# Low halves of 56 weight tiles: an accumulating DMA onto ScalarE's negated high halves, in place of VectorE's subtraction

## The chip, the cores and the metric

The kernel runs on one core of a Trainium2 chip. Its engines have lists of their own and run side by side: TensorE (PE, with its weight load PEld), VectorE (DVE), ScalarE (ACT), GpSimd (POOL), SyncE (SP, which issues the loads). The metric is device time in microseconds. The profile is of one execution.

## The reference

One decoder block on 512 tokens of width 1024, float32. Three token mixers are fed by one projection, merged by sigmoid gates, projected, added; a gated MLP with a short causal convolution follows.

```python
h = rms_norm(x, ln1_g[l]);  z = h @ w_in[l]
z_a, z_b, z_c, z_g = jnp.split(z, split_at, axis=-1)
u, v = jnp.split(jax.nn.gelu(z_a), 2, axis=-1)
v = layer_norm(v, sg_ln_g[l], sg_ln_b[l])
y_a = (u * chunked_spatial_gating(v, sg_w[l], sg_b[l])) @ w_a_out[l]
p, g_lin = jnp.split(z_b, 2, axis=-1)
c = causal_depthwise_conv(p * jax.nn.sigmoid(g_lin), cv_w[l], cv_b[l])      # 31 taps
y_b = jax.nn.silu(layer_norm(c, cv_ln_g[l], cv_ln_b[l])) @ w_b_out[l]
q, k, vv = jnp.split(z_c, 3, axis=-1)                                       # q, k normalised per head
y_c = stick_breaking_attention(q, k, vv) @ w_c_out[l]                       # 8 heads of 64
gates = jax.nn.sigmoid(z_g.reshape(bsz, t, N_BRANCH, d) + b_gate[l])
merged = gates[:, :, 0] * y_a + gates[:, :, 1] * y_b + gates[:, :, 2] * y_c
x = x + merged @ w_out[l]
up = causal_depthwise_conv(rms_norm(x, ln2_g[l]) @ w_up[l], ffn_conv_w[l], ffn_conv_b[l])
gate, val = jnp.split(up, 2, axis=-1)
x = x + (jax.nn.silu(gate) * val) @ w_down[l]
```

## The kernel before

Each float32 matrix product is made of three products of shorter numbers. Every operand is split into a high half (`hi`, rounded to the type float32r) and a low half (`lo`, what the rounding left), and `mm3` issues high times high, high times low and low times high, all into one PSUM tile. A split (`split`) is a copy on ScalarE that rounds, and a subtraction on VectorE.

All weights lie in one array `wall` of 140 tiles of 128x1024, in the order of their use: 8 for the convolution branch's input (`NZB`), 20 for the token projections (`NTOK`: values and gates of the spatial gating, q, k, v), 24 for the gates (`NZG`) and 12 for the branch outputs (`NY`), these two mixed branch by branch, then 8, 44 and 24 for the output projection and the MLP. One weight tile feeds 24 matmuls. `wload` (line 156) fetches and splits a tile: SP loads it into one of two raw buffers (`wr`), ScalarE writes `wh`, VectorE `wl`, each into a buffer of a pool of six, so three weights are held at a time. The copy of weight i waits until PE is done with weight i - 3. `wnext` issues `wload` two weights ahead. Both instructions carry a high priority (`hot`) in the scheduler that puts the written program in its final order.

Work that is not a weight's product is written as generators in queues (`side`): the convolution's taps (`conv`, VectorE), the attention's scores, sigmoids and transposed operands (`soft`, ScalarE, VectorE and PE), its scans (`scan`, VectorE), the transposes and the product with v (`av`, PE, ScalarE and VectorE). A planner sets when they are written: `spend` adds the estimated cost of what was issued to a clock for each engine, and `fill`, called twice per weight, takes the next step of `soft` while the clocks of ScalarE and VectorE are behind PE's, and of `conv` while VectorE's is. A weight was charged `PEU`, `SPD` and `SPA` (PE, VectorE, ScalarE), in two halves. Every engine works off its list in order. POOL's list has the masks of the scores (the affine selects of line 650), which VectorE's line 690 waits for.

The weights 8 to 63 are used in `tok_group` (line 441) and `branch` (line 764). The functions that the change touches:

Of the kernel before, what the change touches and what calls it, by code (L numbers as in the profile page):

```python
# [11 lines left out]
AF = mybir.ActivationFunctionType  # L12
ALU = mybir.AluOpType
# [3 lines left out]
T = 512  # L17
# [21 lines left out]
NZB, NTOK, NZG, NY, NOUT, NUP, NDN = 8, 20, 24, 12, 8, 44, 24  # L39
# [6 lines left out]
def tile_block(ctx: ExitStack, tc: tile.TileContext, xT, x0g, wall, cst, lnv, sgw, outT):  # L46
    nc = tc.nc
    act, dve, pool, pe, sp = nc.scalar, nc.vector, nc.gpsimd, nc.tensor, nc.sync
# [37 lines left out]
    f = lambda ap: ap.bitcast(F32)  # L86
# [16 lines left out]
    def load(out, in_):  # L103
        i = sp.dma_start(out=out, in_=in_)
        after(i, dlast[0])
        dlast[0] = i.ins
# [8 lines left out]
    def split(hi, lo, src):  # L115
        act.copy(out=hi, in_=src)  # L116
        dve.tensor_tensor(out=lo, in0=src, in1=f(hi), op=ALU.subtract)  # L117
# [5 lines left out]
    def mm3(out, ah, al, bh, bl, start, stop, behind=None):  # L123
        i = pe.matmul(out=out, lhsT=ah, rhs=bh, start=start, stop=False)  # L124
        after(i, behind)
        mark[0] = i.ins
        pe.matmul(out=out, lhsT=ah, rhs=bl, start=False, stop=False)  # L127
        pe.matmul(out=out, lhsT=al, rhs=bh, start=False, stop=stop)  # L128
# [9 lines left out]
    def hot():  # L138

        return tc.high_priority(int(HOT * tc.cur_priority))  # L140
# [9 lines left out]
    state = {"next": 0}  # L150
# [2 lines left out]
    WARM = 6  # L153
    CONVF = 1.08

    def wload(i):
        n = 768 if i >= NW - NDN and (i - (NW - NDN)) % 3 == 2 else 1024
        raw = wr.tile([P, 1024], F32, tag="wr", name="wr")
        hi = ws.tile([P, 1024], F32R, tag="w", name="wh")
        lo = ws.tile([P, 1024], F32R, tag="w", name="wl")  # L160
        load(raw[:, :n], wall[i, :, :n])
        with hot():
            split(hi[:, :n], lo[:, :n], raw[:, :n])
        wq[i] = (hi, lo)

    def wnext(i):
        while state["next"] < min(NW, i + 1 + AHEAD):
            wload(state["next"])
            state["next"] += 1
        return wq.pop(i)  # L170
# [6 lines left out]
    def spend(pe=0.0, dve=0.0, act=0.0):  # L177
        clk["pe"] += pe
        clk["dve"] += dve
        clk["act"] += act  # L180
# [14 lines left out]
    def fill():  # L195
        for k in ("dve", "act"):
            clk[k] = max(clk[k], clk["pe"] - 10.0)
        live = {n: bool(side[n]) for n in side}
        while True:
            for n, need in (("hi", ()), ("av", ()), ("scan", ()), ("soft", ("act", "dve")), ("conv", ("dve",))):  # L200
                if live[n] and all(clk[k] < clk["pe"] for k in need):
                    live[n] = step(side[n])
                    break
            else:
                return
# [7 lines left out]
    def ca(n, s=0):  # L213
        return 0.09 + s * 0.09 + n * 0.000833

    def cd(n, s=0):
        return 0.07 + s * 0.06 + n * 0.001042
# [16 lines left out]
    for k in range(KD):  # L234
        i, j = k // 2, half[k % 2]
# [3 lines left out]
        raw, hi, lo = w4[i]  # L239
# [141 lines left out]
    def chan_unit(i, ps, xs):  # L381

        hi, lo = wnext(i)
        for k in range(KD):
            ks = slice(k * P, (k + 1) * P)
            mm3(ps, hi[:, ks], lo[:, ks], xs[k][0], xs[k][1], k == 0, k == KD - 1)
            if k == 3:
                spend(PEU / 2, SPD / 2, SPA / 2)
                fill()
        spend(PEU / 2, SPD / 2, SPA / 2)  # L390

    def group4():
        return [MM(), MM(), Z(), AV()]
# [1 line left out]
    PEU, SPD, SPA = 5.11, cd(1024), ca(1024)  # L395
# [4 lines left out]
    for kk in range(4):  # L400
        hi, lo = wnext(iw)
# [39 lines left out]
    def tok_group(evac, dve_c, act_c):  # L441
        nonlocal iw
        g = group4()
        for kk in range(4):
            hi, lo = wnext(iw)
            iw += 1

            order = [(c, j) for c in range(4) for j in range(2)] if kk == 3 else \
                [(c, j) for j in range(2) for c in range(4)]
            for n, (c, j) in enumerate(order):  # L450
                k = 2 * kk + j
                js = slice(j * 512, (j + 1) * 512)
                cs = slice(c * P, (c + 1) * P)
                xh, xl = xn[k][0][:, cs], xn[k][1][:, cs]
                pe.matmul(out=g[c], lhsT=xh, rhs=hi[:, js], start=k == 0, stop=False)  # L455
                pe.matmul(out=g[c], lhsT=xh, rhs=lo[:, js], start=False, stop=False)  # L456
                mark[0] = pe.matmul(out=g[c], lhsT=xl, rhs=hi[:, js], start=False, stop=k == KD - 1).ins  # L457
                if k == KD - 1:
                    with hot():
                        evac(c, g[c])  # L460
                if n == 3 or n == 7:
                    if n == 7 and kk == 3:
                        spend(0, dve_c, act_c)
                    spend(PEU / 2, SPD / 2, SPA / 2)
                    fill()


# [296 lines left out]
    def branch(b, src, need, first, last):  # L764
        nonlocal iw
        for half in range(2):
            gate = []
            for j in range(4):
                oc = half * 4 + j
                ps = MM()  # L770
                chan_unit(iw, ps, xn)
                iw += 1
                with hot():
                    gate.append(S())
                    table_act(out=gate[j], in_=ps, func=AF.Sigmoid, bias=c_("bg", b * 8 + oc))
                spend(0, 0, ca(T))
                fill()
            finish(*need)
            for i2 in range(2):
                hi, lo = wnext(iw)  # L780
                iw += 1
                for jj in range(2):
                    j = 2 * i2 + jj
                    oc = half * 4 + j
                    ps = MM()
                    for k in range(KW):
                        ks = slice((jj * KW + k) * P, (jj * KW + k + 1) * P)
                        mm3(ps, hi[:, ks], lo[:, ks], src[k][0], src[k][1], k == 0, k == KW - 1)
                    with hot():
                        dve.tensor_tensor(out=gate[j], in0=ps, in1=gate[j], op=ALU.mult)  # L790
                    if first:
                        m[oc] = gate[j]
                    else:
                        dve.tensor_tensor(out=m[oc], in0=m[oc], in1=gate[j], op=ALU.add)  # L794
                    if last:
                        mg[oc] = PR()
                        split(mg[oc][0], mg[oc][1], m[oc])
                    spend(PEU / 2, SPD / 2 + 2 * cd(T), SPA / 2)
                    fill()

    branch(0, uaT, ["hi"], True, False)
# [6 lines left out]
    for oc in range(KD):  # L808
        x1[oc] = S()
        sp.dma_start(out=x1[oc], in_=xT[oc])  # L810
        hi, lo = wnext(iw)
# [18 lines left out]
    for fch in range(KF):  # L830
        cv = []
        pss = []
        for gv in range(2):
            hi, lo = wnext(iw)
# [8 lines left out]
        for gv in range(2):  # L843
# [6 lines left out]
            for s in (1, 2):  # L850
                dve.scalar_tensor_tensor(out=a[:, :T - s], in0=t[:, s:T], scalar=c_("fw", ch * 3 + s),  # L851
                                         in1=a[:, :T - s], op0=ALU.mult, op1=ALU.add)
# [12 lines left out]
    for oc in range(KD):  # L865

        w = {}
        for n in ((slice(0, T),) if oc < KD - 1 else (slice(0, T // 2), slice(T // 2, T))):
            ps = Z()
            for k in range(KF):  # L870
# [3 lines left out]
                hi, lo = w[k // 8]  # L874
# [99 lines left out]
```

## Time and profile before

| | us |
|---|---|
| median of 3 runs (811.57 to 812.11) | 811.88 |
| the profiled execution | 813.14 |
| its span | 810.6 |
| PE busy in the span | 801.5 |
| VectorE, ScalarE, POOL busy | 569.6, 365.6, 26.3 |

The span is the time from the first to the last instruction that the profile records; the rest of the execution lies around it. Busy shares are means over stages that differ: in the first 300 us VectorE is nearly full, later it is not. Matmuls overlap each other, so a row's duration of a matmul is longer than the distance from its start to that of the next.

### The profile page before, as it was taken

The page shows a single profiled execution, that of the slowest core. Times are in us where ns is not written, and L with a number is a line of the kernel's source. Part 1 is how long each engine was busy: PE and PEld are TensorE (multiplying, and loading weights), DVE is VectorE, ACT ScalarE, POOL GpSimd, SP SyncE. Part 2 cuts the span into 40 slices and gives each one's busy share as a digit, 9 for nine tenths or more (in the row PEclk, how much of TensorE's full clock was granted, in tenths as well). Part 3 has the DMA queues.
Part 4 walks back from the last instruction along what each step waited for, and adds up shares of the span by engine and source line. Part 5 has one row for each costly group of instructions (what it writes and reads, how often), then busy time and mean ns, then how long its engine had stood idle before and what let it go on. Part 6 is the DMA issues. An engine that isn't in the chain of part 4 may idle for free.

```text
span 810.6 us, 9429 instructions
## 1 busy us (share of the span) xinstructions
PE 801.5 (99%) x3672; PEld 665.0 (82%) x3672; DVE 569.6 (70%) x772; ACT 365.6 (45%) x526; POOL 26.3 (3%) x44
## 2 busy tenths in 40 slices
PE   9999999998999999999999999999999999999998
PEld 6888888877887888888888888888888888888888
DVE  7799988999899887955556777777777777322221
ACT  7354434687585533643434544444444444211110
POOL 0001000021121100000000000000000000000000
PEclk9999999999999999999999999999999999999999
DMA  7233332212212132232244233223223322333330
GB/s 268 79 128 133 103 102 66 94 55 76 77 54 78 53 105 82 100 104 82 101 168 135 87 104 103 82 102 104 97 85 105 104 84 92 111 104 130 104 105 27
DMA packets 24812, 80.49 MB, mean 99 GB/s; under 512 B 2752, under 2 KB 3392, under 8 KB 24768
## 3 DMA queue, kind: packets, MB, share of 16 engines
q1 hardware_dynamic: 24768, 79.89, 29.4%
q8 instruction: 29, 0.48, 0.3%
q14 instruction: 15, 0.12, 0.0%
HBM read 77.78 MB, written 2.10 MB: 99 GB/s over the span
## 4 chain that ended last, share of the span: by engine, by line
PE 89%; DVE 8%; ACT 2%; issue 1%; DVEq 0%
PE z L124 18%; PE z L127 18%; PE z L128 18%; PE mm L124 7%; PE mm L127 7%; PE mm L128 6%; PE mm L457 2%; PE mm L455 2%; PE mm L456 2%; DVE s L334 2%; DVE h L687 2%; DVE wl L117 2%; PE z L457 1%; PE z L455 1%; PE a L455 1%
## 5 line engine op out<-in xcount | busy, mean ns | idle before, releaser
L116 ACT CAST wh<-wr 128x1024 fp32r<-128x1024 f32 (+1 forms) x136 | 141.7, 1042 | 247.7 <-PE z L127 114.3
L124 PE MATMUL z<-s,wh 128*128 128x512 f32 (+1 forms) x617 | 236.2, 383 | 0.0
L128 PE MATMUL z<-s,wl 128*128 128x512 f32 (+1 forms) x617 | 236.2, 383 | 0.0
L127 PE MATMUL z<-s,wh 128*128 128x512 f32 (+1 forms) x617 | 236.2, 383 | 0.0
L117 DVE TENSOR_TENSOR wl<-wr,wh 128x1024 fp32r<-128x1024 f32 (+1 forms) x136 | 164.6, 1210 | 100.8 <-ACT wh L116 99.2
L128 PEld LDWEIGHTS z<-s,wl 128*128 128x128 f32 x617 | 116.0, 188 | 22.8
L124 PEld LDWEIGHTS z<-s,wh 128*128 128x128 f32 x617 | 116.0, 188 | 22.7
L127 PEld LDWEIGHTS z<-s,wh 128*128 128x128 f32 x617 | 116.0, 188 | 22.6
L124 PE MATMUL mm<-s,wh 128*128 128x512 f32 x302 | 120.5, 399 | 0.0
L127 PE MATMUL mm<-s,wh 128*128 128x512 f32 x302 | 118.2, 391 | 0.0
L128 PE MATMUL mm<-s,wl 128*128 128x512 f32 x302 | 117.7, 392 | 0.0
L334 DVE SCALAR_TENSOR_TENSOR s<-s,cst 128x511 f32<-128x511 f32 (+29 forms) x120 | 82.5, 732 | 1.5 <-ACT s L329 1.3
L128 PEld LDWEIGHTS mm<-s,wl 128*128 128x128 f32 x302 | 57.0, 189 | 12.3
L124 PEld LDWEIGHTS mm<-s,wh 128*128 128x128 f32 x302 | 57.2, 189 | 11.7 <-ACT s L113 0.5
L851 DVE SCALAR_TENSOR_TENSOR h<-h,cst 128x511 f32<-128x511 f32 x88 | 65.7, 747 | 1.5
L127 PEld LDWEIGHTS mm<-s,wh 128*128 128x128 f32 x302 | 57.2, 189 | 11.1 <-DVE s L117 0.2
L848 DVE TENSOR_TENSOR h<-z,rs 128x512 f32<-128x512 f32 x44 | 30.2, 687 | 39.9 <-PE z L128 39.8
L849 ACT ACTIVATE h<-h,cst 128x512 f32<-128x512 f32 x44 | 35.9, 816 | 3.2 <-DVE h L848 3.0
L116 ACT CAST s<-h 128x512 fp32r<-128x512 f32 x18 | 11.2, 620 | 49.1 <-DVE h L856 49.1
L113 ACT ACTIVATE h<-h 128x512 f32<-128x512 f32 x22 | 13.9, 632 | 42.1 <-DVE h L851 42.1
L116 ACT CAST s<-s 128x512 fp32r<-128x512 f32 x29 | 17.5, 620 | 31.9 <-DVE s L794 14.1
L455 PE MATMUL mm<-wh,s 128*128 128x512 f32 x80 | 31.3, 391 | 0.0
(187 smaller groups left out, 882.1 us busy)
## 6 DMA issues: line engine op xcount, KB each, us to landing
wr<-wall SPq DMA_DIRECT2D x128, 512.0 KB, 3.3
s<-xT SPq DMA_DIRECT2D x15, 256.0 KB, 4.1
wr<-wall SPq DMA_DIRECT2D x8, 384.0 KB, 3.0
outT<-s SPq DMA_DIRECT2D x7, 256.0 KB, 2.0
h<-wall SPq DMA_DIRECT2D x3, 512.0 KB, 7.0
s<-lnv SPq DMA_DIRECT2D x2, 256.0 KB, 3.6
s<-sgw SPq DMA_DIRECT2D x2, 256.0 KB, 3.6
x<-x0g SPq DMA_DIRECT2D x1, 260.0 KB, 2.7
```

Of the source, the lines that this page charges most:

```text
L116: act.copy(out=hi, in_=src)
L117: dve.tensor_tensor(out=lo, in0=src, in1=f(hi), op=ALU.subtract)
L124: i = pe.matmul(out=out, lhsT=ah, rhs=bh, start=start, stop=False)
L127: pe.matmul(out=out, lhsT=ah, rhs=bl, start=False, stop=False)
L128: pe.matmul(out=out, lhsT=al, rhs=bh, start=False, stop=stop)
L334: after(dve.scalar_tensor_tensor(out=acc[j][:, :T - s], in0=cc[j][:, s:], scalar=c_("cvw", j * TAPS + s), in1=acc[j][:, :T - s], op0=ALU.m ...
L455: pe.matmul(out=g[c], lhsT=xh, rhs=hi[:, js], start=k == 0, stop=False)
L456: pe.matmul(out=g[c], lhsT=xh, rhs=lo[:, js], start=False, stop=False)
L457: mark[0] = pe.matmul(out=g[c], lhsT=xl, rhs=hi[:, js], start=False, stop=k == KD - 1).ins
L848: dve.tensor_tensor(out=t[:, :T], in0=pss[gv], in1=rs2, op=ALU.mult)
L849: act.activation(out=a, in_=t[:, :T], func=AF.Identity, scale=c_("fw", ch * 3), bias=c_("fb", ch))
L851: dve.scalar_tensor_tensor(out=a[:, :T - s], in0=t[:, s:T], scalar=c_("fw", ch * 3 + s), in1=a[:, :T - s], op0=ALU.mult, op1=ALU.add)
```

## The change

For the 56 weights 8 to 63 the low half is made in another way. ScalarE writes the high half as before, then a second time with the factor -1 into the buffer of the low half. A DMA in POOL's queue reads the weight from HBM again and adds it to that buffer, so that it holds the weight less its high half. The other weights are split as before. The planner's charge for such a weight is 0 for VectorE and twice the old one for ScalarE.

```diff
+    def bydma(i):
+        return NZB <= i < NZB + NTOK + NZG + NY
+
+    def wspend():
+        if bydma(state["next"]):
+            spend(PEU / 2, 0, SPA)
+        else:
+            spend(PEU / 2, SPD / 2, SPA / 2)
...
         load(raw[:, :n], wall[i, :, :n])
         with hot():
-            split(hi[:, :n], lo[:, :n], raw[:, :n])
+            act.copy(out=hi[:, :n], in_=raw[:, :n])
+            if not bydma(i):
+                dve.tensor_tensor(out=lo[:, :n], in0=raw[:, :n], in1=f(hi[:, :n]), op=ALU.subtract)
+            else:
+                act.activation(out=lo[:, :n], in_=f(hi[:, :n]), func=AF.Copy, scale=-1.0)
+                pool.dma_start(out=lo[:, :n], in_=wall[i, :, :n], accum_op=ALU.add)
...
-                spend(PEU / 2, SPD / 2, SPA / 2)
+                wspend()
                 fill()
-        spend(PEU / 2, SPD / 2, SPA / 2)
+        wspend()
...
-                    spend(PEU / 2, SPD / 2 + 2 * cd(T), SPA / 2)
+                    wspend()
+                    spend(0, 2 * cd(T), 0)
                     fill()
```

The lists of the engines move with the planner. In the changed kernel the lines from `wload` on have higher numbers: the copy is L174, VectorE's subtraction L176, the negation L179, the DMA L180, and the lines behind them are 17 higher than before.

ScalarE's list before, in the middle of the attention's stage; `wh` is a weight's high half, `h` the scores' tiles, `s<-z` the split of transposed scores, `s<-mm` a gate's sigmoid:

```order
L116 CAST wh<-wr 128x1024
L116 CAST s<-z 128x128
L113 ACTIVATE s<-mm,cst 128x512
L113 ACTIVATE h<-z,qs 128x512 x2
L113 ACTIVATE h<-z,qs 128x384 x2
L113 ACTIVATE h<-z,qs 128x256 x2
L113 ACTIVATE h<-z,qs 128x128 x2
L116 CAST s<-z 128x512
L116 CAST s<-z 128x384
L116 CAST wh<-wr 128x1024
```

The same stage on ScalarE now; L179 writes the negated half, L371 squares for the convolution's layer norm:

```order
L174 CAST wh<-wr 128x1024
L116 CAST s<-z 128x128
L179 ACTIVATE wl<-wh 128x1024
L113 ACTIVATE s<-mm,cst 128x512
L116 CAST s<-z 128x512
L113 ACTIVATE h<-z,qs 128x512
L116 CAST s<-z 128x384
L113 ACTIVATE h<-z,qs 128x512
L113 ACTIVATE h<-z,qs 128x384 x2
L113 ACTIVATE h<-z,qs 128x256 x2
L113 ACTIVATE h<-z,qs 128x128 x2
L371 ACTIVATE s<-s 128x512 x2
```

The negation stands one to three instructions behind the copy, and the layer norm of the convolution, which stood behind the last head, is drawn into this stage.

POOL's list before, from the end of the start-up on:

```order
L273 MEMSET onesW 128x128
L491 AFFINE_SELECT s<-s 128x512 x2
L659 MEMSET s 128x512
L660 AFFINE_SELECT s<-s 128x128
L650 AFFINE_SELECT h<-h 128x128 x32
```

POOL's list now, from the end of the start-up to the masks of the fourth head (L667, before L650):

```order
L677 AFFINE_SELECT s<-s 128x128
L180 DMA wl<-wall 128x1024 x13
L667 AFFINE_SELECT h<-h 128x128
L180 DMA wl<-wall 128x1024
L667 AFFINE_SELECT h<-h 128x128 x3
L180 DMA wl<-wall 128x1024
L667 AFFINE_SELECT h<-h 128x128
L180 DMA wl<-wall 128x1024
L667 AFFINE_SELECT h<-h 128x128 x4
L180 DMA wl<-wall 128x1024
L667 AFFINE_SELECT h<-h 128x128 x3
```

The DMAs stand between the masks of each head; VectorE's list holds 56 subtractions less, and PE's holds the same matmuls, with the scores and transposes of the attention written earlier (the last head's transposes by about 17 us of PE's work).

## Rows read from the trace of the kernel before

**Rows 1.** The page's first lines: span; busy time and share of each engine.

```profile
span 810.6 us, 9429 instructions
PE 801.5 (99%) x3672; PEld 665.0 (82%) x3672; DVE 569.6 (70%) x772; ACT 365.6 (45%) x526; POOL 26.3 (3%) x44
```

**Rows 2.** Windows: length, busy (x) of PE, PEld, DVE, ACT, POOL, PEclk, DMA, GB/s.

```profile
30.00:150.00 120.00, 120.00 (x550) 100.08 (x549) 111.08 (x171) 56.33 (x82) 3.73 (x4) 1.00 0.30 101
...
180.00:210.00 30.00, 27.64 (x136) 22.75 (x134) 28.65 (x40) 22.80 (x46) 5.98 (x9) 0.94 0.22 71
...
480.00:600.00 120.00, 120.00 (x531) 99.36 (x530) 87.70 (x111) 54.17 (x67) 0.00 (x0) 1.00 0.29 97
153.85:279.39 125.54, 121.30 (x606) 100.60 (x605) 113.34 (x155) 87.19 (x164) 21.55 (x32) 0.99 0.21 68
154.00:248.00 94.00, 90.65 (x452) 74.86 (x451) 86.91 (x118) 70.49 (x131) 15.41 (x24) 0.98 0.20 66
```

**Rows 3.** Timeline of PE: start, duration, line, operation, tiles (x: instructions merged).

```profile
194.41 0.28 PE L713 MATMUL a<-s,b 128*128 128x256 f32 x1
194.53 0.28 PE L714 MATMUL a<-s,b 128*128 128x256 f32 x1
...
194.82 0.41 PE L700 MATMUL z<-ident,h 128*128 128x128 f32 x2
197.56 0.45 PE L700 MATMUL z<-ident,h 128*128 128x128 f32 x1 [2.33 <-DVE s L624]
...
241.31 0.93 PE L700 MATMUL z<-ident,h 128*128 128x128 f32 x7
241.99 0.47 PE L124 MATMUL mm<-s,wh 128*128 128x512 f32 x1
```

**Rows 4.** Chain of waits, 192 to 202: start, duration, engine, tile, line.

```profile
195.39 1.23 DVE wl L117
...
196.65 0.77 DVE s L624
...
198.00 0.43 PE mm L124
```

**Rows 5.** Groups by shape: count | busy us, mean ns | idle before, releasers.

```profile
L117 DVE TENSOR_TENSOR wl<-wr,wh 128x1024 fp32r<-128x1024 f32 x128 | 156.9, 1226 | 100.8 <-ACT wh L116 99.2
L116 ACT CAST wh<-wr 128x1024 fp32r<-128x1024 f32 x128 | 135.0, 1055 | 225.5 <-PE z L127 92.1 <-PE mm L127 44.1 <-issue 42.5
...
L113 ACT ACTIVATE h<-h 128x512 f32<-128x512 f32 x22 | 13.9, 632 | 42.1 <-DVE h L851 42.1
L116 ACT CAST s<-h 128x512 fp32r<-128x512 f32 x18 | 11.2, 620 | 49.1 <-DVE h L856 49.1
```

**Rows 6.** ScalarE's waits, 150 to 280: waiter, releaser: us in total, times, longest.

```profile
ACT s L116 <- DVE s L721: 5.7, 3, 2.8
...
ACT s L626 <- DVE s L624: 3.3, 3, 1.7
```

**Rows 7.** The page's DMA queue (share of 16 engines) and issues (us to landing).

```profile
q1 hardware_dynamic: 24768, 79.89, 29.4%
...
wr<-wall SPq DMA_DIRECT2D x128, 512.0 KB, 3.3
...
h<-wall SPq DMA_DIRECT2D x3, 512.0 KB, 7.0
```

**Rows 8.** Groups by shape, POOL.

```profile
L650 POOL TENSOR_SCALAR_AFFINE_SELECT h<-h 128x128 f32<-128x128 f32 x32 | 21.6, 682 | 173.9 <-ACT h L113 173.7
...
masks.py:199 POOL TENSOR_SCALAR_AFFINE_SELECT ident<-ident 128x128 f32<-128x128 f32 x1 | 0.3, 292 | 0.0
```

**Rows 9.** Timeline of ScalarE, casts of weights 28 and 29; in brackets the wait.

```profile
148.41 1.06 ACT L116 CAST wh<-wr 128x1024 fp32r<-128x1024 f32 x1 [1.81 <-PE a L456]
...
153.85 1.05 ACT L116 CAST wh<-wr 128x1024 fp32r<-128x1024 f32 x1 [4.00 <-PE a L456]
```

More of the change, by code (lines that the diff above doesn't have):

```diff
@@ L463, in tok_group @@
                         spend(0, dve_c, act_c)
-                    spend(PEU / 2, SPD / 2, SPA / 2)
+                    wspend()
                     fill()
@@ L797, in branch @@
                         split(mg[oc][0], mg[oc][1], m[oc])
-                    spend(PEU / 2, SPD / 2 + 2 * cd(T), SPA / 2)
+                    wspend()
+                    spend(0, 2 * cd(T), 0)
                     fill()
```

## The prediction, made before the changed kernel ran

> **What bounds the kernel now.** I read the page first. The profiled execution took 813.14 us with a span of 810.6, so 2.5 us lie around the span, and it stands 1.3 us above the median of 811.88. TensorE (PE) is busy for 801.5 of 810.6 us [rows 1]: no change on another engine can give back more than what PE loses somewhere. The table by stages says where that is [rows 2]. From 30 to 150 us, and from 480 to 600, PE is never idle; the later stretch has 531 matmuls in 120.00 us, a pace of 0.226 us for one of 512 columns. The loss lies between about 150 and 280, where the attention's scores, scans and transposes run beside the gates. From the cast of the 29th weight tile at 153.85 to that of the 45th at 279.39 are 125.54 us. In the order of before, PE's list between the matmuls that release these two casts holds 413 matmuls of 512 columns, 30 of 384, 30 of 256 and 124 of 128. The first cost 0.227; two of 256 start 0.12 apart, and seven transposes of 128 take from 241.31 to 241.99, 0.10 each, [rows 3]; I take 0.118 and 0.105, and 0.172 for 384 by interpolation. That is 115.5 us of work, so this stage loses 10.1 us. Of them 4.2 show as idle PE (121.30 busy), and some 1.8 as clock: the granted clock is 0.94 in 180 to 210 [rows 2]. The rest is matmuls that start late and overlap nothing.
>
> Why PE waits there is seen around 195: a transpose stands idle for 2.33 us until 197.56, for VectorE's L624 of the next pair of heads [rows 3] (a PSUM tile has to come free), and the chain of waits has the subtraction of a weight's low half, 1.23 us, on VectorE right ahead of that L624 [rows 4]. Behind this stop a step of PE takes 0.43 us in the chain instead of 0.23: the lower of the clock's two levels, 1.2 instead of 2.4 GHz. VectorE is busy for 86.9 of the 94.0 us from 154 to 248, ScalarE for 70.5 [rows 2].
>
> **What the change takes off VectorE.** The 56 weight tiles 8 to 63 lose their subtraction of 1.226 us [rows 5]: 68.7 us off VectorE. From 30 to 150 and after 280 that is worth nothing, since PE loses nothing there. In the stage it counts, but not in full, because the planner now charges VectorE nothing for these weights and fills it with other work. Adding the durations over VectorE's list in the two orders, from the scan of head 0 to that of head 7, gives 102 us before (14 subtractions of weights, 17.2 us, and 23 convolution taps among them) and 83.5 after (no subtraction, 8 taps, and a part of the convolution's layer norm). PE's work between is some 10% less, so VectorE goes from full to about nine tenths. Of the 10.1 us I leave 1.5 for stops on VectorE that remain.
>
> **What it adds to ScalarE.** One pass of 128x1024 per weight, from SBUF to SBUF with a constant scale. The trace has no such row: at 512 columns the activation from SBUF takes 632 ns and the cast 620, and the cast of 1024 takes 1055 [rows 5], so 1.07, with 1.055 and 1.3 (twice 632) as ends. Outside the stage it hides in ScalarE's idle time (56.3 busy of 120 from 30 to 150). In the stage it doesn't. ScalarE's list between the casts of weights 29 and 41 has 133 instructions before and 171 after: 12 negations and 26 others that the planner pulled forward. The row of 154 to 248 has 131 instructions in 70.5 us, 0.54 each. So 70.5 + 12.8 + 14.0 = 97.3 us of ScalarE stand against PE work of 92.6 (319, 28, 26 and 117 matmuls of the four widths). ScalarE becomes the full engine of this stretch and ends it 4.7 us behind. To that come its waits in list order for VectorE, 5.7 and 3.3 us in before [rows 6]; with VectorE less full I keep half, 4.5. Its waits for PE fall away once it is late. Lag at weight 41: 9.2 us, with 4.7 and 13.7 as ends.
>
> **What it adds behind ScalarE.** The low half is now ready only after a DMA from POOL's queue that waits for the negation, reads the weight again from HBM, reads the negated half and writes the sum. No row shows one. A plain load of the same 512 KB lands 3.3 us after its issue, and 7.0 in the crowded first stretch [rows 7]. The queue's packets took 29.4% of 810.6 us for 79.89 MB, or 1.56 us for 512 KB. I count 3.3, once 1.56 for the second stream, once 1.56 because the plain load of the weight after next starts as the cast ends and shares the engines, and 0.7 for the issue by the affine select, POOL's nearest instruction [rows 8]: 7.1 us, with 3.3 and 9.3 (7.0 + 1.56 + 0.7) as ends.
>
> The Trainium skill puts a plain transfer issued by POOL at 2.0 us plus bytes over 436 GB/s (DMA: Bandwidth & Descriptors, section Anatomy of one DMA). For 512 KB that is 3.2, an estimate that agrees with the row of 3.3; with the second stream it would be 4.4, and by it the sum below would come out 2.7 us lower. The rows show no accumulating transfer, so I stay with 7.1.
>
> POOL's list is in order, so the affine selects of the scores now queue behind these DMAs, and VectorE's L690 behind them. Each waits on ScalarE's sigmoid that stands behind the same negation, so I count nothing; if the DMA's issue alone held POOL, it would be one affine select's 0.7 us per head. SP's list hardly moves.
>
> **The room, and the sum.** A weight's buffers come free when PE is done with the weight three before it: casts that wait for PE start 5.44 apart [rows 9]. In a plain stretch that leaves two weights, 10.9 us, and 0.45 until the low half is read; cast, sigmoid of a gate and negation use up 2.0 to 2.7, so 8.7 to 9.3 are left for the DMA. 7.1 fits, and PE loses nothing there. At weight 41 the order has 53 matmuls of 512 columns, 4 of 384, 4 of 256 and 17 of 128 between release and first use: 15.0 us. Less the lag of 9.2 and 2.65 for cast and negation, plus 0.45, 3.6 are left: the DMA is 3.5 us late and PE stops that long, once, since each stop gives ScalarE its time back. Stage loss after: 3.5 + 1.5 = 5.0 instead of 10.1. The profiled execution would take 813.14 - 5.1 = 808.0, the median 811.88 - 5.1 = **806.8**.
>
> **Rivals.**
> - *Slower: the DMA takes longer than the room.* It decides from about 8.9 us on, in the 33 plain weights (8 to 19, 24 to 26, 46 to 63). A chain C from release to data, and PE's 5.45 on the weight, share three slots, so a weight takes (C + 5.45)/3. With C = 2.4 - 0.45 + DMA, 10 us makes 5.80, or 0.35 x 33 = 11.5 us; the stage loses 2.9 more: 821. At 12 us it is 845. For it: nothing in this trace shows such a transfer, and a POOL instruction here takes 682 ns beside a full VectorE, against 292 at the start for the same tile shape [rows 8]. Against it: the DMA engines are busy for 0.3 of their time [rows 2].
>   On these 292 and 682 ns bears the Trainium skill (SBUF — State Buffer, section Who interferes with whom): a VectorE instruction with two SBUF inputs and a POOL instruction that reads SBUF shut each other out, and a VectorE in a two-port mode keeps POOL from writing descriptors. The two rows agree with the first. If issuing suffered as the affine select does, the DMA would come to 7.5 and the sum 0.4 higher; the second would need the two-port mode, and the page denies that to tensor_tensor.
> - *Slower, by ScalarE alone.* If all its waits for VectorE stay and the pass takes 1.3, the lag at weight 41 is 16.5 (13.7 and 12 times 0.23) and the stop 11.0; with 1.5 from VectorE the stage loses 12.5: 814.3.
> - *No change: the planner gives it all back.* If VectorE's new work stops PE as the subtractions did, 5 to 6.7 stay from VectorE on top of 3.5: 8.5 to 10.2, or 810.3 to 812. Against it stand 83.5 us where 102 were.
> - *Faster in full.* DMA of 3.3 to 4.4 and few waits: no loss but VectorE's, 803 to 804, and 801.8 if nothing is lost.
>
> **How the numbers follow.** My forecast 0.42, faster in full 0.15, no change 0.13, the long DMA 0.20, ScalarE alone 0.10. A difference of 0.2% (1.6 us) is about what a measurement of this kernel can tell from none. Faster 0.57, same 0.13, slower 0.30. The likeliest case alone, with faster in full, spans 802 to 810. Over all, 802 to 822 leaves out the DMA beyond 10 us and what little is below.
>
> **What would show it.** Right: VectorE's list without 56 subtractions, ScalarE 60 us busier; PE's loss between 150 and 280 near 5 us, its last stops on a low half late from the DMA or on ScalarE; from issue to landing about 7 us. Wrong: idle PE between 30 and 150 or after 290 (the DMA is over 9 us), or stops at VectorE's L624 and L721 (the lines of before) of the old size.

## The result: slower, 834.49 us

The changed kernel takes 834.49 us (median; 834.15 to 835.67) against 811.88: a ratio of 1.0271, with a 95% interval of 1.0253 to 1.0288. Forecast were 806.8 with a range of 802 to 822. The profiled execution took 834.72 us with a span of 832.9. From here on a line number of the changed kernel is that of before plus 17, beyond the weights' own lines: L174 casts the high half, L176 subtracts (80 weights are left to it), L179 negates, L180 issues the accumulating DMA. In the experiments the numbers shift again by a few lines.

The page's first lines, its software queue and two of its issues, which answer to [rows 1, 7]:

```profile
span 832.9 us, 9545 instructions
...
PE 804.1 (97%) x3672; PEld 666.4 (80%) x3672; DVE 505.5 (61%) x716; ACT 419.0 (50%) x582; POOL 79.7 (10%) x100
...
q0 software_dynamic: 8064, 29.36, 21.2%
...
wr<-wall SPq DMA_DIRECT2D x128, 512.0 KB, 3.3
wl<-wall POOLq DMA_DIRECT2D x56, 512.0 KB, 5.5
```

VectorE is 64.1 us less busy and ScalarE 53.4 us more. The new transfer lands 5.5 us after its issue, less than the 7.1 that I counted. Nothing of this says where 22 us went. The groups by shape of the new and the delayed instructions (count, busy us, mean ns, idle before) hold the first hint, in POOL's two selects of the masks, the masks of the spatial gating's weights `sgw` (L508; 1287 ns in the mean before, 6403 now; the last line is that of before):

```profile
L179 ACT ACTIVATE wl<-wh 128x1024 fp32r<-128x1024 f32 x56 | 59.2, 1056 | 0.7
...
L180 POOL DMA_DIRECT2D wl<-wall x56 | 48.7, 871 | 296.7 <-ACT wl L179 273.8 <-ACT y L113 10.2 <-ACT s L116 7.2
L667 POOL TENSOR_SCALAR_AFFINE_SELECT h<-h 128x128 f32<-128x128 f32 x32 | 17.1, 608 | 28.2 <-ACT h L113 28.0
L508 POOL TENSOR_SCALAR_AFFINE_SELECT s<-s 128x512 f32<-128x512 f32 x2 | 12.8, 6403 | 7.5 <-DMA s<-sgw 7.5
...
L491 POOL TENSOR_SCALAR_AFFINE_SELECT s<-s 128x512 f32<-128x512 f32 x2 | 2.6, 1287 | 76.8 <-DMA s<-sgw 62.1 <-DVE mv L499 14.7
```

The windows of the changed kernel, with the columns of [rows 2], say in which stretch it is lost:

```profile
60.00:90.00 30.00, 19.25 (x77) 15.37 (x76) 23.51 (x40) 9.97 (x12) 14.39 (x4) 0.83 0.54 137
...
150.00:300.00 150.00, 137.69 (x674) 113.55 (x674) 124.66 (x191) 125.61 (x217) 32.46 (x50) 0.98 0.59 129
...
480.00:600.00 120.00, 120.00 (x531) 99.34 (x531) 88.60 (x112) 56.40 (x70) 0.00 (x0) 1.00 0.29 97
```

and the row of before for the stage:

```profile
150.00:300.00 150.00, 145.76 (x720) 120.62 (x719) 134.72 (x189) 96.43 (x177) 21.55 (x32) 0.99 0.22 71
```

The late stretch is as it was. One loss is between 60 and 90 us, where before lost nothing, and one in the stage, where PE is busy for 8 us less than before while ScalarE carries 125.6 us of the 150 instead of 96.4. To size both I use one measure below, "PE's loss". It takes the steps from one matmul's start to the next that are longer than 0.24 us, and sums what they exceed 0.228 us by, so that the half clock behind a stop counts too (but not what narrow matmuls lose at it). It is 14.3 us in before and 36.3 after, 22.0 more, which is the difference of the spans (22.3). Of the 36.3, 12.9 lie in 60 to 90 and 19.6 in 150 to 300 (before: 0.0 and 9.7).

**The stop at 72 to 83 us.** The timeline of VectorE, POOL, ScalarE and PE, in this order (start, duration, engine, line; in brackets the idle time before and its releaser):

```profile
58.51 19.66 DVE L351 SCALAR_TENSOR_TENSOR s<-s,cst 128x510 f32<-128x510 f32 x30
...
66.83 11.83 POOL L508 TENSOR_SCALAR_AFFINE_SELECT s<-s 128x512 f32<-128x512 f32 x1 [7.47 <-DMA s<-sgw]
78.62 0.88 POOL L180 DMA_DIRECT2D wl<-wall  x1
...
78.70 0.62 ACT L116 CAST s<-s 128x512 fp32r<-128x512 f32 x1 [15.05 <-POOL s L508]
...
83.31 0.79 PE L472 MATMUL mm<-wh,s 128*128 128x512 f32 x1 [10.75 <-ACT b L113]
```

VectorE has no subtractions of weights in its list here, so it runs 30 convolution taps in a row, from 58.51 to 78.17. POOL's select of the second mask starts at 66.83 in the middle of them and ends at 78.66, 0.5 us after the last tap. The mask's cast heads ScalarE's list and waits 15 us; behind it in order stand a weight's cast and negation, a table load and the two evacuations (L113) that give PE a PSUM tile back. PE stands idle for 10.75 us and then runs at the lower clock for some matmuls, at 0.43 us a step; the granted clock of the stretch is 0.83. In the kernel before the same select took this long, with VectorE's list beside it:

```profile
63.72 1.53 POOL L491 TENSOR_SCALAR_AFFINE_SELECT s<-s 128x512 f32<-128x512 f32 x1 [62.10 <-DMA s<-sgw]
...
58.91 4.70 DVE L334 SCALAR_TENSOR_TENSOR s<-s,cst 128x511 f32<-128x511 f32 x7
63.53 1.22 DVE L117 TENSOR_TENSOR wl<-wr,wh 128x1024 fp32r<-128x1024 f32 x1
64.66 5.05 DVE L334 SCALAR_TENSOR_TENSOR s<-s,cst 128x508 f32<-128x508 f32 x7
```

VectorE had no idle time there either. What broke its taps into runs of six or seven were the subtractions: the select starts beside one (63.53 to 64.75) and ends at 65.25, 0.5 us after it, while the first tap behind takes longer.

**The stage.** The waits of PE from 150 to 300 us in the changed kernel (waiter, releaser: us in total, times, longest):

```profile
PE z L717 <- DVE s L641: 6.5, 3, 2.5
PE mm L124 <- ACT s L113: 2.8, 1, 2.8
PE a L730 <- DVE s L738: 1.4, 1, 1.4
```

No wait is for a low half or its DMA. The first line is the stop of [rows 3] under its new numbers, three times instead of once (6.5 us instead of 2.3); the second is a PSUM tile that ScalarE evacuates late. All waits of PE in the stage come to 12.3 us; the rest of the 19.6 are late starts and steps at the lower clock.

Why VectorE's L641 comes late shows in part in VectorE's own waits for ScalarE in the stage, the first two lines now, the others before:

```profile
DVE s L117 <- ACT s L116: 6.9, 9, 1.7
DVE h L704 <- ACT h L113: 5.6, 3, 2.9
...
DVE s L117 <- ACT s L116: 1.7, 3, 0.7
DVE h L687 <- ACT h L113: 0.5, 1, 0.5
```

and in the window between the two casts for which the prediction counted 171 instructions of ScalarE (weights 29 and 41):

```profile
173.26:284.11 110.85, 99.04 (x490) 81.48 (x489) 92.45 (x135) 97.07 (x172) 27.25 (x44) 0.97 0.52 115
```

ScalarE is busy for 97.07 us of it, as forecast (97.3), and idle for 13.8. Of these it waits 8.1 for VectorE and 4.6 for PE.

### The profile page after: what moved, and what is told of

Read it like the earlier page. It is cut to its first block, busy times and chain, and to the rows that moved or that the text cites. A ratio compares the mean times of both kernels' runs of the same rounds, so it can differ in the third digit from the quotient of the medians.

```text
span 832.9 us, 9545 instructions
## 1 busy us (share of the span) xinstructions
PE 804.1 (97%) x3672; PEld 666.4 (80%) x3672; DVE 505.5 (61%) x716; ACT 419.0 (50%) x582; POOL 79.7 (10%) x100
## 4 chain that ended last, share of the span: by engine, by line
PE 83%; DVE 8%; ACT 3%; DMA 2%; POOL 2%; issue 1%; SPq 0%; DVEq 0%; ACTq 0%
PE z L124 17%; PE z L127 17%; PE z L128 17%; PE mm L128 6%; PE mm L124 6%; PE mm L127 6%; DVE h L704 2%; PE mm L472 2%; PE mm L473 2%; PE mm L474 2%; POOL s L508 1%; DVE s L351 1%; DMA s<-sgw 1%; DVE h L707 1%; PE z L473 1%
## 5 line engine op out<-in xcount | busy, mean ns | idle before, releaser
L174 ACT CAST wh<-wr 128x1024 fp32r<-128x1024 f32 (+1 forms) x136 | 141.6, 1041 | 230.0 <-PE z L127 114.8
L176 DVE TENSOR_TENSOR wl<-wr,wh 128x1024 fp32r<-128x1024 f32 (+1 forms) x80 | 95.8, 1198 | 87.4 <-ACT wh L174 86.1
L351 DVE SCALAR_TENSOR_TENSOR s<-s,cst 128x511 f32<-128x511 f32 (+29 forms) x120 | 80.4, 726 | 0.1
L180 POOL DMA_DIRECT2D wl<-wall x56 | 48.7, 871 | 296.7 <-ACT wl L179 273.8
L179 ACT ACTIVATE wl<-wh 128x1024 fp32r<-128x1024 f32 x56 | 59.2, 1056 | 0.7
L807 DVE TENSOR_TENSOR s<-mm,s 128x512 f32<-128x512 f32 x24 | 16.5, 688 | 64.6 <-PE mm L128 64.5
```

The costliest lines, as they stand in the source:

```text
L174: act.copy(out=hi[:, :n], in_=raw[:, :n])
L176: dve.tensor_tensor(out=lo[:, :n], in0=raw[:, :n], in1=f(hi[:, :n]), op=ALU.subtract)
L179: act.activation(out=lo[:, :n], in_=f(hi[:, :n]), func=AF.Copy, scale=-1.0)
L180: pool.dma_start(out=lo[:, :n], in_=wall[i, :, :n], accum_op=ALU.add)
L351: after(dve.scalar_tensor_tensor(out=acc[j][:, :T - s], in0=cc[j][:, s:], scalar=c_("cvw", j * TAPS + s), in1=acc[j][:, :T - s], op0=ALU.m ...
```

## The experiments

Theory A: the stop at 72 to 83 is POOL's select, shut out of SBUF while VectorE runs instructions with two SBUF inputs, with ScalarE's list in order behind it. Theory D: the stage loses its 10 us because the planner, which charges VectorE nothing for these weights, draws other work together there, beside ScalarE's second pass. The rivals were that the DMA itself does it, or ScalarE's pass alone. The measured times stand together here; the ratio is to the kernel before on the same chip (where its median was 811.5 to 812.2), with its interval, and the last columns are PE's loss in us from 0 to 150 and from 150 to 300, and busy ScalarE and VectorE in the stage.

| kernel | median us | ratio | 0-150 | stage | ACT | DVE |
|---|---|---|---|---|---|---|
| before | 811.9 | 1 | 4.4 | 9.7 | 96.4 | 134.7 |
| after | 834.49 | 1.0271 (1.0253-1.0288) | 16.7 | 19.6 | 125.6 | 124.7 |
| masks early | 826.3 | 1.0176 (1.0157-1.0196) | 7.6 | 19.7 | 122.9 | 116.3 |
| one-input taps | 821.58, one run | | 3.0 | 20.3 | 122.5 | 114.7 |
| old charges | 811.31 | 0.9999 (0.9987-1.0011) | 6.4 | 8.9 | 115.8 | 112.1 |
| outside the stage | 815.54 | 1.0051 (1.0036-1.0066) | 5.0 | 9.8 | 102.5 | 127.4 |
| layer norm held | 823.68 | 1.0135 (1.0119-1.0150) | 5.7 | 18.5 | 124.2 | 113.8 |
| old charges, masks early | 813.35 | 1.0020 (1.0011-1.0028) | 5.6 | 8.9 | 115.9 | 112.2 |
| half charge | 827.13 | 1.0182 (1.0168-1.0196) | 4.8 | 18.3 | 120.5 | 114.9 |
| no negation | 808.46 | 0.9953 (0.9940-0.9967) | 5.2 | 5.5 | 96.6 | 116.2 |
| order alone | 833.66 | 1.0257 (1.0240-1.0274) | 11.0 | 21.1 | 107.7 | 144.2 |
| stage only | 810.72 | 0.9985 (0.9976-0.9995) | 4.4 | 8.7 | 113.6 | 115.5 |
| GpSimd negates | 825.39 | 1.0154 (1.0139-1.0170) | 19.0 | 7.0 | 101.0 | 120.1 |
| GpSimd, stage only | 809.12 | 0.9964 (0.9952-0.9976) | 3.6 | 7.5 | 96.3 | 121.6 |

**Masks early.** The two loads and selects of the masks move to the program's start.

```diff
+    sgraw = []
+    for i in range(2):
+        raw = S((P, 4, P))
+        load(raw, sgw[:, i * 4:(i + 1) * 4])
+        pool.affine_select(out=raw, in_=raw, pattern=[[0, 4], [-1, P]], compare_op=ALU.is_ge,
+                           fill=0.0, base=0, channel_multiplier=1)
+        sgraw.append(raw)
...
-            raw = S((P, 4, P))
-            sp.dma_start(out=raw, in_=sgw[:, i * 4:(i + 1) * 4])
-            pool.affine_select(out=raw, in_=raw, pattern=[[0, 4], [-1, P]], compare_op=ALU.is_ge,
-                               fill=0.0, base=0, channel_multiplier=1)
+            raw = sgraw[i]
```

> The changed kernel with the two loads of sgw and their affine selects (L508) moved to the start of the program, ahead of the first DMA of POOL and of the run of convolution taps. Theory A (the stop of 11 us between 72 and 83 comes from the affine select, which 30 taps of VectorE in a row keep out of SBUF for 11.8 us, and from ScalarE's list that stands behind its cast): the selects take 1 to 1.5 us, PE's loss between 60 and 90 goes from 12.9 to under 1, the time from 834.5 to 821 to 823. Rival B (the stop comes from the accumulating DMAs of these weights being late): the loss stays where it is, 833 to 836.

The stretch from 60 to 90 us, in the windows of this run:

```profile
60.00:90.00 30.00, 30.00 (x134) 24.86 (x133) 29.45 (x51) 18.18 (x21) 5.58 (x8) 1.00 0.88 200
```

The stop is gone, though the DMA engines are busier in this stretch than in the changed kernel, 0.88 against 0.54. The gain is 8 us and not 13, so the time misses its range, since 2.4 us are now lost at 30 to 60 and 1.4 more at the start; the masks' loads stand ahead of most weights' there, but that they cause it is not shown. The stage is untouched, at 19.7.

**One-input taps.** The select stays where it was, but the first 19 taps of two of the four channel tiles become a statistics instruction that reads one tile, so the convolution lacks them.

```diff
-                after(dve.scalar_tensor_tensor(
+                if j < 2 and s < 20:
+                    after(dve.bn_stats(out=scr, in_=cc[j]), mark[0])
+                else:
+                    after(dve.scalar_tensor_tensor(
```

> The changed kernel in which the first 19 taps of convolution channels 0 and 1 are replaced by a statistics instruction on 512 columns with one SBUF input (the convolution lacks these taps). VectorE's list is as dense as before. Theory A (two SBUF inputs shut POOL's reads out): the select at 67 us takes 1 to 2 us, PE loses under 1 us between 60 and 90, 821 to 824. Rival C (POOL is slow there because its own DMAs are being written or land): the select still takes about 12 us, and the time stays at 832 to 836.

The selects in the groups by shape of this run:

```profile
L513 POOL TENSOR_SCALAR_AFFINE_SELECT s<-s 128x512 f32<-128x512 f32 x2 | 1.3, 633 | 3.9 <-DMA s<-sgw 3.9
```

633 ns instead of 6403 at the same place in POOL's list, and PE loses 0.1 us at 60 to 90: it is the taps, not the place and not the load. By the rule of the Trainium skill that the prediction weighed (SBUF — State Buffer, section Who interferes with whom) the cause is the taps' second SBUF input, and the run agrees. It doesn't single that input out, since the statistics instruction also writes 6 columns where a tap writes some 500. For its two-port case the Trainium skill, in the same section, lets the loser wait until the other's instruction ends; here the select of 11.83 us stood through some 17 taps (19.66 us for 30 is 0.66 a tap), and what was measured decides.

**Old charges.** The order's planner charges half a subtraction to VectorE and one pass to ScalarE, as before; DMA and negation stay.

```diff
-        if bydma(state["next"]):
-            spend(PEU / 2, 0, SPA)
-        else:
-            spend(PEU / 2, SPD / 2, SPA / 2)
+        spend(PEU / 2, SPD / 2, SPA / 2)
```

> The changed kernel with the planner's charges of before for every weight (VectorE one subtraction, ScalarE one pass). Theory D (both losses come from work that the new charges pull forward: 30 taps in a row at 60, a full ScalarE in the attention's stage): VectorE's list keeps gaps, the select takes 1 to 3 us, PE loses under 1 us between 60 and 90 and 4 to 10 in the stage: 805 to 812. Rival E (the second pass on ScalarE costs the stage its 20 us whatever the planner does): 60 to 90 without loss, the stage 18 to 22: 820 to 823.

Its trace, first the stage, then the masks' selects, their mean and each beside VectorE's taps:

```profile
150.00:300.00 150.00, 144.93 (x723) 120.17 (x722) 112.11 (x168) 115.75 (x199) 39.04 (x52) 1.00 0.66 143
```

```profile
L505 POOL TENSOR_SCALAR_AFFINE_SELECT s<-s 128x512 f32<-128x512 f32 x2 | 1.6, 803 | 7.4 <-DMA s<-sgw 7.4
...
59.22 9.04 DVE L348 SCALAR_TENSOR_TENSOR s<-s,cst 128x511 f32<-128x511 f32 x13 [0.27 <-ACT s L343]
68.66 0.63 POOL L505 TENSOR_SCALAR_AFFINE_SELECT s<-s 128x512 f32<-128x512 f32 x1 [7.37 <-DMA s<-sgw]
...
70.59 5.12 DVE L348 SCALAR_TENSOR_TENSOR s<-s,cst 128x505 f32<-128x505 f32 x6
72.85 0.97 POOL L505 TENSOR_SCALAR_AFFINE_SELECT s<-s 128x512 f32<-128x512 f32 x1
```

With the planner's few lines put back, all 22 us are gone, from both places, but for 1.2 at 60 to 90. The first select comes 0.4 us after a run of 13 taps. The second comes within a run of six and takes 0.97 us, while one tap takes 1.81: a run doesn't hold a select off in every case. All 56 transfers and negations are still there; together with VectorE's relief they come to nothing.

**Order alone.** The converse: the new charges and so nearly the changed kernel's order, but the work of before, a subtraction on VectorE.

```diff
-            if not bydma(i):
+            if True:
```

> The changed kernel's order (the planner charges VectorE nothing and ScalarE double for the 56 weights), but the work of before: VectorE subtracts, ScalarE neither negates nor does GpSimd issue a DMA. Theory M, the order alone costs the stage its ten microseconds: VectorE carries 1.23 us per weight that the order doesn't know of, TensorE loses 8 to 14 us more than before between 150 and 300, and the masks' selects don't stop it (the taps wait on weights again), so 819 to 826. Rival N, the order costs only together with ScalarE's second pass: the stage loses within 3 us of before's 9.9, so 810 to 815.

Two stretches of its windows:

```profile
90.00:150.00 60.00, 55.23 (x252) 45.94 (x251) 59.74 (x101) 23.27 (x36) 0.00 (x0) 0.94 0.23 76
150.00:300.00 150.00, 135.07 (x662) 110.61 (x661) 144.20 (x209) 107.66 (x196) 20.32 (x32) 0.97 0.19 62
```

and the largest of PE's waits in the stage:

```profile
PE z L717 <- DVE h L707: 7.4, 1, 7.4
```

The order alone costs 21 us, more than the 819 to 826 I had written, because PE also loses 6.0 at 90 to 150. By the ratios, the new work is worth nothing that can be measured with the old charges (0.9999), and some 1 us the wrong way with the new ones (1.0271 for 1.0257, with intervals that overlap). This doesn't make the two losses one: here VectorE is full (144.2 of 150), and PE's largest stop is for the product behind a head's scans; in the changed kernel neither ScalarE nor VectorE is full (125.6 and 124.7), and its stops are of 2 to 3 us. There is no stop at 60 to 90 here, where the subtractions stand between the taps. What is common is the planner's order, and not even all of it: 113 of PE's 3672 matmuls stand elsewhere than in the changed kernel, most of them between 166 and 204 us, where the stop of 7.4 lies.

**Outside the stage.** Masks early; DMA and the new charges for the weights 8 to 27 and 46 to 63 only.

```diff
-        return NZB <= i < NZB + NTOK + NZG + NY
+        return NZB <= i < NZB + NTOK + NZG + NY and not 28 <= i < 46
```

> As e1_mask_early, with the DMA and the new charges only for the weights 8 to 27 and 46 to 63, outside the attention's stage; 28 to 45 are split as before. Theory (all that e1 still loses against the kernel before is lost by the weights in the stage): PE loses 8 to 12 us between 150 and 300, 809 to 814. Rival (convolution pulled forward before the stage, or the DMAs outside it, cost it): 816 or more.

The stage is back at 9.8, so the weights used in it, with their charges, make its loss. The time is above the expected range, with 2.1 us lost behind 300 where before lost 0.2.

**Layer norm held.** Masks early, new charges, but the convolution's layer norm may not start before the eighth head's transposes are in the list.

```diff
     def convln_gen():
+        while turned[0] < NH:
+            yield NEXT
```

> As e1_mask_early (826.3 us, 19.7 us of PE's time lost between 150 and 300), but the layer norm of the convolution may not start before the transposes of the eighth head are written, so that its squares, table loads and sums leave ScalarE's and VectorE's lists in the attention's stage. The zero charge for VectorE stays. Theory F (of the stage's extra loss a good part is the layer norm, which the zero charge drew in): the stage loses 12 to 16, 819 to 823. Rival G (the loss is the heads standing closer: the last transposes come 90 us of PE's work after the first, 103 in before): 18 to 21, 825 to 828.

ScalarE's timeline around its largest stop, and PE's:

```profile
302.95 0.62 ACT L116 CAST s<-s 128x512 fp32r<-128x512 f32 x1 [1.36 <-DVE s L402]
303.47 1.26 ACT L113 ACTIVATE s<-mm,cst 128x512 f32<-128x512 f32 x2
...
304.21 0.80 PE L124 MATMUL mm<-s,wh 128*128 128x512 f32 x1 [6.82 <-ACT s L113]
```

Held back, the layer norm costs in one piece nearly what it cost in parts: PE's loss from 180 to 270 falls from 15.4 (masks early) to 7.4, but a stop of 7 us stands at 297. It has the make of the first one: an evacuation of PSUM that stands in ScalarE's list behind a cast, and the cast waits for VectorE. The stage's 18.5, in which this stop is counted, lies in the rival's range, and the time between the two ranges.

**Half charge.** Masks early, and half of the old share charged to VectorE.

```diff
-            spend(PEU / 2, 0, SPA)
+            spend(PEU / 2, SPD / 4, SPA)
```

> As e1_mask_early, with half a subtraction charged to VectorE for each weight instead of none. PE's list then has the last transposes of the heads where before has them and the sums of the layer norm at 265 and 274 us of PE's work (before 305 and 314, e1 206 and 229). Theory F with G (the zero charge costs by drawing the norm in and the heads together): the stage loses 9 to 13, 811 to 815. Rival (the second pass on ScalarE costs more the more of it is honestly charged): 818 or more.

The theory behind my number fell, and the time lies in the rival's range. The heads' transposes stand where they stood in before, yet PE stops behind a matmul at 297.7 as in the run above:

```profile
305.48 0.80 PE L124 MATMUL mm<-s,wh 128*128 128x512 f32 x1 [7.44 <-ACT s L113]
```

In both runs the plan ends the layer norm by here; with the old charges VectorE reads the norm's two column sums some 40 us later, at 322.6 and 331.4 instead of 282.2 and 294.0, and PE loses nothing behind 300. Which charge is right, other than the old one, I have not found.

**Old charges, masks early**, and the same **without the negation**, where the low half is a plain copy by DMA.

```diff
-                act.activation(out=lo[:, :n], in_=f(hi[:, :n]), func=AF.Copy, scale=-1.0)
-                pool.dma_start(out=lo[:, :n], in_=wall[i, :, :n], accum_op=ALU.add)
+                pool.dma_start(out=lo[:, :n], in_=wall[i, :, :n])
```

> The changed kernel with the planner's old charges (as e3_old_charges, 811.3 us) and the affine selects at the start (as e1_mask_early). All 56 weights go by negation and DMA. Theory: what e3 lost between 60 and 90, 1.2 us, goes, the stage loses 8 to 10 as in e3: 809.5 to 811. Rival (the loads of sgw in the start-up cost as much as they save): 811 to 812.5.

> As e9_old_early without the negation: the DMA of POOL writes the plain weight into the low half's buffer (the low halves of these 56 weights are wrong). ScalarE has the load of before, VectorE 68.7 us less than before, the DMA stays. Theory H (the gain from VectorE's relief is eaten by ScalarE's second pass in the stage): PE loses 2 to 5 us in the stage, 803 to 806. Rival I (what is left are waits of the heads' own chain over ScalarE, VectorE and PE, which neither pass sets): 7 to 10 us stay, 808 to 811.

Early masks bring nothing once the order is right: 813.35, slightly slower than before and outside both ranges. The profiled span (811.2) is shorter than that with late masks (812.0), but the latter is of the slowest of ten executions (813.91, the median is 811.31), so it doesn't speak against the medians; what makes the difference stays open. The second run's time is in its rival's range, and its loss in the stage between the two. It tells where the expected gain went. The stage of both:

```profile
150.00:300.00 150.00, 144.96 (x723) 120.16 (x722) 112.19 (x167) 115.93 (x200) 38.93 (x52) 1.00 0.64 143
...
150.00:300.00 150.00, 148.05 (x740) 123.42 (x739) 116.22 (x171) 96.63 (x178) 33.41 (x53) 1.00 0.44 148
```

VectorE relieved, ScalarE as in before: PE's loss in the stage is 5.5. With the negation it is 8.9. So VectorE's relief wins 4.2 of the 9.7, and the negation gives 3.4 back (with what the accumulation adds to the DMA, 5.4 us to landing instead of 3.6; with the sum, PE waits at most 0.7 us for one).

**Stage only.** Old charges, late masks; DMA and negation for the weights 28 to 45.

```diff
-        return NZB <= i < NZB + NTOK + NZG + NY
+        return 28 <= i < 46
```

> The DMA and the negation only for the weights 28 to 45, which are used in the stage, with the planner's old charges; all others are subtracted by VectorE, masks as before. If what is left of the old charges' loss outside the stage comes from the negations there (0.8 us more at the start, 1.2 at 60 to 90), it goes, and the stage keeps about 9: 810 to 811.5. If the stage does not gain from VectorE's relief because ScalarE's pass takes it away, also there no more than 1 us is won: not under 810. Rival: ScalarE, late in the stage from subtractions still queued on VectorE, costs more: 813 or more.

810.72, 0.15% below before: clear of 1 by its interval, but not under the 810 of the expectation. The stage's 8.7 is that of all 56 (8.9). So outside the stage nothing is won by the change, and in it the relief of the one engine is the load of the other.

**GpSimd negates**, all 56 weights with old charges and early masks, and then **in the stage only**, with late masks.

```diff
-                act.activation(out=lo[:, :n], in_=f(hi[:, :n]), func=AF.Copy, scale=-1.0)
+                pool.tensor_scalar(out=lo[:, :n], in0=f(hi[:, :n]), scalar1=-1.0, scalar2=None, op0=ALU.mult)
```

> Old charges and early masks, but GpSimd negates the 56 high halves, not ScalarE. Theory K: ScalarE's 59 us of negations are what separates the run with them (813.4) from the run without (808.5), and GpSimd, busy 39 of the stage's 150 us, has room for them: 807 to 810, faster than before. Rival L: GpSimd's passes over 128x1024 are locked out behind VectorE's two-input instructions as the selects were, the weights and the masks of the heads, which stand in the same list, come late: 814 to 830.

VectorE, POOL and PE in the run with all 56:

```profile
82.58 11.08 DVE L356 SCALAR_TENSOR_TENSOR s<-s,cst 128x501 f32<-128x501 f32 x17
...
84.14 12.14 POOL L176 TENSOR_SCALAR wl<-wh 128x1024 fp32r<-128x1024 f32 x1 [1.48 <-ACT wh L171]
...
101.86 0.80 PE L478 MATMUL mm<-wl,s 128*128 128x512 f32 x1 [7.63 <-DMA wl<-wall]
```

The lock again, foretold this time by the rival: one negation, 3.1 us in the mean, takes 12.14 behind 17 taps, ends 2.6 us after the last, and PE waits 7.63 us for the DMA behind it (and 1.97 for another, at 54). In the stage PE loses 7.0, less than with ScalarE's negation. So the last run keeps GpSimd to the stage:

> GpSimd negates, and only for the weights 28 to 45 of the stage; old charges, all other weights subtracted by VectorE. Theory K: both VectorE and ScalarE are relieved where TensorE loses its 9.9 us, and nothing is changed elsewhere: 806.5 to 810. Rival L (GpSimd locked out, masks of the heads late in its list): 813 to 822.

```profile
150.00:300.00 150.00, 146.19 (x731) 121.68 (x730) 121.64 (x173) 96.34 (x177) 88.75 (x68) 1.00 0.57 136
```

```profile
L176 POOL TENSOR_SCALAR wl<-wh 128x1024 fp32r<-128x1024 f32 x18 | 56.0, 3111 | 105.9 <-PE z L624 72.8 <-ACT wh L171 33.1
```

809.12 us, faster than both kernels: 0.9964 of before (0.9952 to 0.9976). PE's loss in the stage falls by 2.2, and by 0.8 at the start, where the two kernels are alike; the second part is not the change's. VectorE and ScalarE are both no busier than in before, and GpSimd, busy for 88.8 us of 150, does the pass; none of its 18 negations takes longer than 4.04 us, and no run of taps in the stage longer than 4.32 us, five taps.

## Why the prediction was wrong

- **VectorE's relief: its load right, its worth twice too high.** 56 times 1.226 were to go, 64.1 us went. In the stage the relief was to leave "1.5 for stops on VectorE that remain" of 10.1. With the old charges and ScalarE left alone 5.5 of 9.7 stay, so it is worth 4.2 and not 8.6. In the changed kernel the sign that I gave for this came: the stops at L624 (now L641) grew from 2.3 to 6.5 us, those at L721 (now L738) kept their size, 1.5 and 1.4.
- **ScalarE's pass: price and load right, its waits wrong.** 1.07 for one forecast, 1.056 measured; 97.3 us of ScalarE between two casts forecast, 97.07 measured. But I kept 4.5 us of waits for VectorE and let those for PE fall away; measured are 8.1 and 4.6. So the stretch takes 110.9 us against PE work of 92.6, 18 us of lag and not 9.2.
- **The DMA: right in what it decides.** 7.1 forecast, 5.5 measured, inside 3.3 to 9.3; the one wait for it that the trace shows before a weight's use is 0.2 us, for one of the 56. The rival of the long DMA held the measured time in its 821 to 845, but by a mechanism that isn't there.
- **POOL's list: wrong, and one of the two failures.** "Each waits on ScalarE's sigmoid that stands behind the same negation, so I count nothing", at most 0.7 us per head. I looked at the selects of the scores alone and not at the two of the masks, and I priced the lock by one instruction, 292 against 682 ns. Here its price was what was left of the run of taps, 11.8 us, and the change made that run: it took out the subtractions that stood between the taps, and its order put 30 of them together (with the old charges the run is 13, with the subtractions left in at most seven). From 30 to 150 I had written that VectorE's relief "is worth nothing, since PE loses nothing there"; with this order it was worth 12.9 us the wrong way. The masks early and the one-input taps show this cause. The sign I gave for being wrong, idle PE between 30 and 150, came, but I had tied it to a DMA of over 9 us.
- **The stage's sum: wrong, the other failure.** 1.5 for VectorE and 3.5 once for a low half, 5.0 in all; measured are 19.6, none of it for a low half. The lag of ScalarE I let end in one stop that "gives ScalarE its time back". In fact ScalarE and VectorE wait for each other in list order, and PE stops for both, at L641 (6.5) and at evacuations (2.8). I had counted the work that the planner pulls forward as load on ScalarE, and not asked what else a plan that believes VectorE free puts side by side. The old charges show that the loss goes with the order; the order alone loses as much with the old work, by other stops. Which pieces of the order make the 19.6 stays open: the layer norm and the heads' places, tried one at a time, did not settle it.
- **"No change: the planner gives it all back" was the nearest rival in kind**, and I held against it that VectorE's list between two scans was shorter. A shorter list on one engine says nothing of the other two.
- The forecast's own mechanism, with the order kept, would have gained nothing that can be measured (the old charges, 0.9999), not 5.1: in the stage VectorE gives 4.2 and ScalarE takes 3.4. That the 3.4 is near my 3.5 is luck, since hardly any of it is a wait for a low half.

How a charge of zero, and one of a half, lead the planner to the layer norm's new place is read from the orders alone, and was not taken apart further.

## What to carry to other kernels

When a change to a scheduled kernel also changes the planner's costs, run the new work in the old order and the old work in the new order before pricing any instruction: here the work was worth some 1 us at most and the order over 20. Moving a pass from a full engine to the next fullest one won nothing here; on the idle one it won some 2 us, where that engine's known collision was rare. And taking one kind of instruction out of an engine's list lengthens the runs of the others: ask who got in only between them.

## What of the hardware was unexpected

- A GpSimd instruction that reads SBUF can stand until a run of VectorE instructions with two SBUF inputs ends: a select 11.83 us, through the last 17 of 30 taps, and a negation 12.14 beside 17 taps, against 0.63 for the same select beside one-input instructions. It isn't always so: with the old charges a select within six taps took 0.97.
- GpSimd's issue of an accumulating DMA shows no such delay: 871 ns in the mean over 56 issues, 862 to 1013; the 13 that stand beside taps took 862 to 886.
- An accumulating DMA of 512 KB, HBM onto SBUF, lands in 5.5 us (5.1 to 8.1) where a plain load takes 3.3, and a plain copy from POOL's queue 3.6 (no negation); a negation of 128x1024 takes 1.06 us on ScalarE and 3.11 on GpSimd.
